# Half of the output columns moved beside the last delta rule heads, eight more merge columns in pairs, and early copies of transposed keys and values, in a one-core encoder layer

## The chip, the cores and the metric

The kernel runs on one NeuronCore of one Trainium2 chip, in one launch. The metric is the device time of one execution in microseconds. The kernel before takes 2275.59 us (median of three executions, 2275.45 to 2276.55).

## The reference, cut to what matters

One encoder layer is computed for 640 tokens (512 of a prompt, 128 of eight short requests), all in fp32, with 2048 channels:

```
z  = x @ w_in                      # q, k, v, gates, delta-rule q|k|v, two merge gates m_a, m_b (2048 columns each)
y_a = (fox_attention(...) * silu(gate_a)) @ w_out_fox      # 1024 -> 2048
y_b = (delta_rule(...)    * silu(gate_b)) @ w_out_gdn      # 1024 -> 2048
h  = (sigmoid(m_a) * y_a + sigmoid(m_b) * y_b) @ w_out
x1 = layer_norm(alpha * x + h)
out = x1 + sigmoid(x1 @ w_pl_gate) * rms_norm(p @ w_pl_proj)
```

The delta rule has 8 heads of width 128. Each head normalizes its queries and keys to unit length, scales keys and values by factors of its tokens, solves small triangular systems in blocks of 128 tokens, and carries a state from block to block.

## The kernel before, in words

**Columns.** Activations lie with channels on the 128 partitions and the 640 tokens along the free dimension, as 16 tiles (the list `self.op`). A "column" is 128 output channels: `column` runs 16 steps, one for each 128 input channels, and each step has 6 matmuls (`mm6`, L307 and L308). The 6 come from fp32 being split in two parts, high and low (weights `wh`, `wl`, activations `xh`, `xl`): high times high, high times low, low times high, each in two halves of 320 tokens. A column is 96 matmuls of 128x320 and needs 1 MB of weights. The two accumulators of a column lie in two of four PSUM banks `g`.

**Pairs.** Columns computed by `pair` (L381) are done two at a time by Strassen's scheme on 2x2 blocks, with 7 products in place of 8: 168 matmuls of 128x320 for two columns in place of 192. VectorE forms sums of weight halves (L243) and of results. In the kernel before 4 pairs are attention gate columns and 6 pairs are merge columns, that is 12 of the 32 merge columns (`FRONT`); they run in the first stage, while nothing else needs TensorE.

**Weights.** `w_ahead` runs before every step. It starts the DMA of the next half column (512 KB, L223, issued on SyncE) into one of three `wr` buffers, and splits pieces of it (four steps of a column) on ScalarE (`wh`, L253) and VectorE (`wl`, L254), at most five pieces ahead of TensorE.

**Lanes.** Work beside the columns is written as generators that a list of lanes steps once for every step of a column (`tick`). The engines execute in the order in which this planner writes instructions; it estimates the time of VectorE and ScalarE, but waits in the program are for the real results. In the delta rule stage (`phase_gdn`), each head has 4 columns (query, key, value, gate) and one merge column as filling (`FILL`); after head 7 there are 8 merge columns, beside which the chain of head 7 runs, and 2 more that load and split the 16 operand tiles of the output columns from DRAM (`ogd`).

**The delta rule of one head.** `gdn` transposes the keys (tile `pk`, L779, four 128x128 blocks of the prompt), then one block each of keys, values and queries (`pd`, L784 to L786), then four of queries (`pq`, L792), through four small PSUM banks `s`. The sums of squares (L781, L787, L788, L794) come straight from PSUM on ScalarE. VectorE then makes the inverse roots and the factors `cs` (L816 to L825). Only then ScalarE copies the keys out of `pk` and `pd`, scaled by `cs` (L829 to L831), and TensorE transposes the values (`pv`, L835), which ScalarE copies scaled (L837). The end of the previous head (`gdn_out`: L934, L938) takes two banks of the same four in between. `gdn_blocks` and `gdn_chunks` follow in other lanes.

**Output columns.** `tail` runs 16 columns with 16 steps each: steps 0 to 7 are the attention half, steps 8 to 15 the delta rule half, each in its own pair of banks. After each half VectorE multiplies the accumulator by its merge gate (L1511, two instructions of 128x320), and adds both (L1517). The gates come from DRAM (`md`, two tiles of 320 KB for each column, L1490). Then follow 16 columns with `w_out` and 16 with `w_pl_gate`.

Of the kernel before, what the change touches and what calls it, by code (L numbers as in the profile page):

```python
# [47 lines left out]
class Kernel:  # L48
# [8 lines left out]
    FRONT = 32 - 13 - 7  # L57
# [252 lines left out]
    def column(self, cols=1, each=None, groups=((0, 16),), after=None, modk=False, done=None):  # L310
# [6 lines left out]
        for n0, n1 in groups:  # L317
            ps = [tuple(self.gps(x.stop - x.start) for x in self.cut) for _ in range(cols)]
            for s in range(n0, n1):
                if each:  # L320
                    each(s)
                self.w_ahead()
                for x in range(cols):
                    self.mm6(ps[x], self.wk(c + x, s), self.op[(s - n0) % KT if modk else s], s == n0, s == n1 - 1)
# [445 lines left out]
    def gdn(self, h, kq, v):  # L770
# [5 lines left out]
        junk = self.zt([P, P], "junk")  # L776
        pk = self.sps()
# [15 lines left out]
        for t in range(4):  # L793
            nc.scalar.activation(junk, pq[:, t * P:(t + 1) * P], AF.Square, accum_out=ss[:, 5 + t:6 + t])  # L794

# [30 lines left out]
        kt = self.zt([P, 5, P], "kt", 2)  # L826
        vr = self.zt([P, 5, P], "vr", 2)
        for t in range(4):
            nc.scalar.mul(kt[:, t, :], pk[:, t * P:(t + 1) * P], cs[:, 3, t:t + 1])  # L829
        nc.scalar.mul(kt[:, 4, :], pd[:, 0:P], cs[:, 3, 4:5])  # L830
        nc.scalar.mul(vr[:, 4, :], pd[:, P:2 * P], cs[:, 0, 4:5])  # L831
        yield 2
        pv = self.sps()
        for t in range(4):
            nc.tensor.transpose(pv[:, t * P:(t + 1) * P], v[:, t * P:(t + 1) * P], self.ident)  # L835
# [75 lines left out]
    def gdn_out(self, h, ob, cs):  # L911
# [30 lines left out]
        nc.sync.dma_start(out=self.ogd[8 + h], in_=og)  # L942
# [405 lines left out]
    def phase_gdn(self, conv, work):  # L1348
# [13 lines left out]
        for h in range(H):  # L1362
# [16 lines left out]
            for _ in range(self.FILL if h < 7 else 8):  # L1379
                self.mcol("cth")  # L1380
        self.paced = False
        nc.sync.dma_start(out=self.o["conv"], in_=self.tails)

        raw, nop = {}, [None] * KT
        kq = self.kqs[0]
        tiles = [kq[:, 0, :], kq[:, 1, :]]
        tiles += [self.zt([P, T], t, n, "ogr") for t, n in (("strip", 1), ("cy", 1), ("sg", 1), ("v", 1), ("dt", 1))]

        def load(k):
            raw[k] = tiles[k % 7]  # L1390
            nc.sync.dma_start(out=raw[k], in_=self.ogd[k])

        def each1(s):
            if s >= 9:
                load(s - 9)

        def after(s):
            nop[s] = self.split(raw[s])
            if s + 7 == 15:
                self.until(lambda: self.gdone == 7)  # L1400
            if s + 7 < KT:
                load(s + 7)
        self.mcol("cth", each=each1)
        self.mcol("cth", after=after)
        self.op = nop

    def proj(self, m, op):
# [7 lines left out]
        self.column(groups=tuple((2 * g, 2 * g + 2) for g in range(8)), modk=True, done=fin)  # L1415
# [22 lines left out]
    def rstd(self, acc1, acc2, eps, out, mean=None):  # L1438
# [16 lines left out]
        if acc1 is not None:  # L1455
            m = self.zt([P, 160], "rm")
# [24 lines left out]
    def tail(self):  # L1481
# [5 lines left out]
        def load(n):  # L1487
            for x in range(2):
                ld[n, x] = self.zt([P, T], "ld", 4, "sab")
                nc.sync.dma_start(out=ld[n, x], in_=self.md[2 * n + x])  # L1490
# [3 lines left out]
        for n in range(16):  # L1494
            def each(s):
                if s == 1 and n < 15:
                    load(n + 1)
                if s == 1 and n == 1:
                    self.work["gens"].append(self.rstd(None, re, RMS_EPS, re))

            def after(s):
                if n == 15 and s % 3:
                    k = s - 1 - s // 3
                    nop[k] = self.split(mg[k])
            sab = [ld[n, 0], ld[n, 1]]

            def gated(ps):
                x = sab[len(gs)]
                gs.append(x)
                for hf, sl in enumerate((a, b)):  # L1510
                    nc.vector.scalar_tensor_tensor(out=x[:, sl], in0=x[:, sl], scalar=1.0, in1=ps[hf],  # L1511
                                                   op0=ALU.add, op1=ALU.mult)
            gs = []
            self.column(groups=((0, 8), (8, 16)), each=each, after=after, done=gated)
            sa, sb = gs
            m = self.zt([P, T], "m", 16, "mg")
            nc.vector.tensor_tensor(out=m, in0=sa, in1=sb, op=ALU.add)  # L1517
            mg.append(m)
# [7 lines left out]
        def xload(n):  # L1526
            xr[n] = self.zt([P, T], "ld", 4, "xr")
# [19 lines left out]
        for n in range(16):  # L1547
            def each(s):
                if n == 0 and s < 6:
                    nop[10 + s] = self.split(mg[10 + s])  # L1550
# [39 lines left out]
        def eload(n):  # L1590
            el[n] = self.zt([P, T], "ld", 4, "el")
# [108 lines left out]
def _layout(a):  # L1700
# [30 lines left out]
    bl += list(_wblock(np.concatenate([a["w_out_fox"][0], a["w_out_gdn"][0]], 0)))  # L1731
# [68 lines left out]
```

## Time and profile before

| | |
|---|---|
| median of 3 executions | 2275.59 us |
| the profiled execution's own time | 2279.4 us |
| its span, first to last instruction | 2277.6 us |
| mean granted TensorE clock | 0.998 |
| TensorE busy | 2257.4 us |
| VectorE busy | 1292.8 us |
| ScalarE busy | 802.7 us |
| mean DMA rate over the span | 129 GB/s |

In a profile PE is TensorE's matmuls, PEld its weight loads, DVE VectorE, ACT ScalarE, POOL GpSimd and SP SyncE, which issues all DMAs here. Times of rows are us from the start of the span, durations of one instruction ns. In a group `out<-in` names the tiles, `xN` counts instructions; "idle before" is the time in which the engine stood still ahead of them, followed by what ended it. A row of the waits names the waiting instruction, the one it waited for, the sum in us, how often, and the longest. Busy TensorE time is modelled, since matmuls overlap: a 128x320 matmul lasts 0.31 us and the next one starts about 0.15 us after it.

The stages by time: front columns to 99 us, pairs from 99 to 347 us, attention to about 740 us, then a projection, delta rule heads from 770 to about 1430 us, merge columns beside the end of head 7 to 1590 us, output columns from 1590 to 1815 us, then `w_out` and `w_pl_gate`.

### The profile page before, as it was taken

Reading aid. Unit: us, or ns where it says so; the run is one execution under the profiler, and the core shown is the slowest. Engines: PE = TensorE matmul, PEld = TensorE weight load, DVE = VectorE, ACT = ScalarE, POOL = GpSimd, SP = SyncE. Lnnn points to the kernel's source line nnn. Section 1 sums busy time; section 2 is a strip of 40 time slices with the busy share of each in tenths; the row PEclk is TensorE's granted clock in tenths of the full one; section 3 lists DMA queues with packets and bytes.
Section 4 is the critical chain, followed back from the end, with each engine's and each line's share of the span. In section 5 each row is a group of like instructions: output and inputs, shape, how many; then the busy total and the mean of one; then the engine's idle time right before and its main releaser. Section 6 shows DMA issues by size and latency. Waiting matters only on the chain. (4 is left out here: it accounts for less than half of the span.)

```text
span 2277.6 us, 39935 instructions
## 1 busy us (share of the span) xinstructions
PE 2257.4 (99%) x16034; PEld 2168.6 (95%) x16034; DVE 1292.8 (57%) x2787; ACT 802.7 (35%) x1782; POOL 63.6 (3%) x230
## 2 busy tenths in 40 slices
PE   9999999999999999999999999999999999999999
PEld 7899998978899999999999999999999999999999
DVE  5867664343444547667667667555433533657665
ACT  4444443333333543344344344324111311333222
POOL 0000000000000000000000000000000000020000
PEclk9999999999999999999999999999999999999999
DMA  6333336555654522232233332335433332323331
GB/s 224 125 114 103 123 126 219 201 198 196 198 184 163 182 87 95 91 114 95 95 108 101 97 99 92 115 108 208 150 124 123 104 106 96 100 88 115 121 121 69
DMA packets 114057, 294.72 MB, mean 129 GB/s; under 512 B 22201, under 2 KB 30473, under 8 KB 113873
## 3 DMA queue, kind: packets, MB, share of 16 engines
q1 hardware_dynamic: 113872, 292.18, 38.7%
q8 instruction: 126, 2.06, 0.4%
q14 instruction: 59, 0.48, 0.1%
HBM read 245.23 MB, written 46.90 MB: 128 GB/s over the span
## 5 line engine op out<-in xcount | busy, mean ns | idle before, releaser
L254 DVE TENSOR_TENSOR wl<-wr,wh 128x512 fp32r<-128x512 f32 x564 | 386.9, 691 | 556.1 <-ACT wh L253 542.1
L307 PE MATMUL g<-xh,wh 128*128 128x320 f32 (+1 forms) x1840 | 595.4, 324 | 0.2 <-ACT wh L253 0.2
L307 PE MATMUL g<-xl,wh 128*128 128x320 f32 (+1 forms) x1840 | 569.8, 310 | 0.6 <-DVE xl L282 0.6
L308 PE MATMUL g<-xh,wh 128*128 128x320 f32 x1840 | 569.3, 309 | 0.0
L308 PE MATMUL g<-xl,wh 128*128 128x320 f32 x1840 | 569.1, 309 | 0.0
L307 PE MATMUL g<-xh,wl 128*128 128x320 f32 (+1 forms) x1840 | 569.0, 309 | 0.0
L308 PE MATMUL g<-xh,wl 128*128 128x320 f32 x1840 | 568.5, 309 | 0.0
L253 ACT CAST wh<-wr 128x512 fp32r<-128x512 f32 x564 | 346.8, 620 | 619.8 <-PE g L308 545.9
L307 PEld LDWEIGHTS g<-xh,wh 128*128 128x128 f32 x1840 | 347.3, 189 | 17.6 <-issue 12.7
L307 PEld LDWEIGHTS g<-xl,wh 128*128 128x128 f32 x1840 | 347.0, 189 | 1.1 <-DVE xl L282 1.1
L308 PEld LDWEIGHTS g<-xh,wh 128*128 128x128 f32 x1840 | 347.0, 189 | 0.7
L308 PEld LDWEIGHTS g<-xl,wh 128*128 128x128 f32 x1840 | 346.9, 189 | 0.0
L307 PEld LDWEIGHTS g<-xh,wl 128*128 128x128 f32 x1840 | 346.4, 188 | 0.1
L308 PEld LDWEIGHTS g<-xh,wl 128*128 128x128 f32 x1840 | 346.0, 188 | 0.0
L381 PE MATMUL g<-xh,wh 128*128 128x320 f32 x320 | 99.0, 309 | 1.2 <-ACT u L391 1.2
L381 PE MATMUL g<-xh,wl 128*128 128x320 f32 x320 | 99.0, 309 | 0.0
L381 PE MATMUL g<-xl,wh 128*128 128x320 f32 x320 | 98.9, 309 | 0.0
L254 DVE TENSOR_TENSOR wl<-sr,wh 128x512 fp32r<-128x512 f32 x80 | 53.9, 690 | 41.1 <-ACT wh L253 40.9
L881 DVE TENSOR_TENSOR sx<-sx,sx 80x240 f32<-80x240 f32 (+14 forms) x240 | 68.3, 284 | 8.2
L879 DVE TENSOR_TENSOR sx<-sx,lanes 80x240 f32<-80x240 f32 (+14 forms) x240 | 67.8, 282 | 4.7
L1511 DVE SCALAR_TENSOR_TENSOR sab<-sab,g 128x320 f32<-128x320 f32 x64 | 28.3, 484 | 69.2 <-PE g L307 64.3
L751 DVE SCALAR_TENSOR_TENSOR cy<-strip,taps,cy 128x664 f32<-128x664 f32 x72 | 66.2, 920 | 1.3
(386 smaller groups left out, 2720.3 us busy)
## 6 DMA issues: line engine op xcount, KB each, us to landing
wr<-in_w SPq DMA_DIRECT2D x280, 512.0 KB
kc<-in_kc SPq DMA_DIRECT2D x32, 512.0 KB
vc<-in_vc SPq DMA_DIRECT2D x32, 512.0 KB
xr<-in_xT SPq DMA_DIRECT2D x32, 320.0 KB
md<-m SPq DMA_DIRECT2D x32, 320.0 KB
sab<-md SPq DMA_DIRECT2D x32, 320.0 KB
sr<-in_w SPq DMA_DIRECT2D x10, 512.0 KB
ogd<-og SPq DMA_DIRECT2D x16, 320.0 KB
```

The costliest lines, as they stand in the source:

```text
L253: nc.scalar.copy(out=hi, in_=src)
L254: nc.vector.tensor_tensor(out=lo, in0=src, in1=hi.bitcast(F32), op=ALU.subtract)
L307: nc.tensor.matmul(ps[0], whl[w], xhl[o][:, a], start=(first and x == 0), stop=(last and x == 2))
L308: nc.tensor.matmul(ps[1], whl[w], xhl[o][:, b], start=(first and x == 0), stop=(last and x == 2))
L381: nc.tensor.matmul(ps, a[:, w], b, start=(k == 0 and n == 0 and not more), stop=(k == 7 and n == 2), skip_group_check=True)
L751: nc.vector.scalar_tensor_tensor(out=y[:, 0:CV], in0=strip[:, i:i + CV], scalar=tp[:, 4 * ct + i:4 * ct + i + 1], in1=y[:, 0:CV], op0=ALU. ...
L879: nc.vector.tensor_tensor(out=tmp[:, :, 0:n], in0=xo[:, :, j:j + 1].to_broadcast([80, 8, n]), in1=lanes[:, j:j + 1, j + 1:32].to_broadcast ...
L881: nc.vector.tensor_tensor(out=x[:, :, j + 1:32], in0=xo[:, :, j + 1:32], in1=tmp[:, :, 0:n], op=ALU.subtract)
L1511: nc.vector.scalar_tensor_tensor(out=x[:, sl], in0=x[:, sl], scalar=1.0, in1=ps[hf], op0=ALU.add, op1=ALU.mult)
```

## The change

It has four parts.

1. `FRONT` goes from 12 to 20: 20 merge columns run as 10 pairs, so there are 14 pairs in place of 10.
2. The 8 merge columns after head 7 are gone. The two that load and split operands move to right behind head 7, and split the 8 attention tiles alone (`take`, three tiles of staging in turn). Then 8 weight columns follow, each of which holds the attention halves of two output columns (16 steps in two groups of 8, on operands 0 to 7). ScalarE copies each result out of PSUM (`kept`), and a DMA writes it to DRAM (`fd`). Meanwhile each delta rule tile is loaded and split when its head is done; head 7's goes from VectorE straight into the operand list.
3. `tail` has 8 weight columns in place of 16, with the delta rule halves of two output columns each (operands 8 to 15). For every group of 8 steps it loads three tiles (attention result and two gates) in place of two for 16 steps; VectorE gates the attention result ahead of the end of the group, then the other result, and adds. Eight of the 16 merged tiles are split along the way.
4. In `gdn` ScalarE copies transposed keys and values out of PSUM at once and unscaled (128x512 in one instruction), takes the keys' sums of squares from that copy, and scales keys and values in place in SBUF once `cs` is there. The transposes of the values stand ahead of the factors. There are more steps between these parts.

```diff
-    FRONT = 32 - 13 - 7
+    FRONT = 32 - 5 - 7
...
         pk = self.sps()
         for t in range(4):
             nc.tensor.transpose(pk[:, t * P:(t + 1) * P], kq[:, 0, t * P:(t + 1) * P], self.ident)
-        for t in range(4):
-            nc.scalar.activation(junk, pk[:, t * P:(t + 1) * P], AF.Square, accum_out=ss[:, t:t + 1])
+        nc.scalar.copy(out=kt[:, 0:4, :], in_=pk.rearrange("p (a b) -> p a b", b=P))
         yield
...
-        nc.scalar.activation(junk, pd[:, 0:P], AF.Square, accum_out=ss[:, 4:5])
+        nc.scalar.copy(out=kt[:, 4, :], in_=pd[:, 0:P])
+        nc.scalar.copy(out=vr[:, 4, :], in_=pd[:, P:2 * P])
         nc.scalar.activation(junk, pd[:, 2 * P:3 * P], AF.Square, accum_out=ss[:, 9:10])
+        yield
+        for t in range(5):
+            nc.scalar.activation(junk, kt[:, t, :], AF.Square, accum_out=ss[:, t:t + 1])
         yield
         pq = self.sps()
...
+        yield
+        pv = self.sps()
+        for t in range(4):
+            nc.tensor.transpose(pv[:, t * P:(t + 1) * P], v[:, t * P:(t + 1) * P], self.ident)
+        nc.scalar.copy(out=vr[:, 0:4, :], in_=pv.rearrange("p (a b) -> p a b", b=P))
...
-        for t in range(4):
-            nc.scalar.mul(kt[:, t, :], pk[:, t * P:(t + 1) * P], cs[:, 3, t:t + 1])
-        nc.scalar.mul(kt[:, 4, :], pd[:, 0:P], cs[:, 3, 4:5])
-        nc.scalar.mul(vr[:, 4, :], pd[:, P:2 * P], cs[:, 0, 4:5])
-        yield 2
-        pv = self.sps()
-        for t in range(4):
-            nc.tensor.transpose(pv[:, t * P:(t + 1) * P], v[:, t * P:(t + 1) * P], self.ident)
-        for t in range(4):
-            nc.scalar.mul(vr[:, t, :], pv[:, t * P:(t + 1) * P], cs[:, 0, t:t + 1])
-        yield 3
+        yield 2
+        for t in range(5):
+            nc.scalar.mul(kt[:, t, :], kt[:, t, :], cs[:, 3, t:t + 1])
+        for t in range(5):
+            nc.scalar.mul(vr[:, t, :], vr[:, t, :], cs[:, 0, t:t + 1])
+        yield 2
...
-            for _ in range(self.FILL if h < 7 else 8):
+            for _ in range(self.FILL if h < 7 else 0):
                 self.mcol("cth")
...
+        def kept(ps):
+            t = self.zt([P, T], ("strip", "cy")[self.nf % 2], 1, "fx")
+            for hf in range(2):
+                nc.scalar.copy(out=t[:, hf * HALF:(hf + 1) * HALF], in_=ps[hf])
+            nc.sync.dma_start(out=self.fd[self.nf], in_=t)
+            self.nf += 1
+        for n in range(8):
+            def each(s):
+                while n == 0 and due and (due[0][0] <= self.now or due[0][1] <= s):
+                    take()
+                k = 8 + n
+                if s == 1 and n < 7:
+                    self.until(lambda: self.gdone >= n)
+                    load(k, ("sg", "cth")[n % 2])
+                if s == 13 and n < 7:
+                    nop[k] = self.split(raw[k])
+            self.column(groups=((0, 8), (8, 16)), base=0, each=each, done=kept)
...
+            for x, d in enumerate((self.fd[n], self.md[2 * n], self.md[2 * n + 1])):
+                ld[n, x] = self.zt([P, T], "ld", 6, "sab")
+                nc.sync.dma_start(out=ld[n, x], in_=d)
...
+        def gated(ps):
+            n = len(mg)
+            x = ld[n, 2]
+            for hf, sl in enumerate((a, b)):
+                nc.vector.scalar_tensor_tensor(out=x[:, sl], in0=x[:, sl], scalar=1.0, in1=ps[hf],
+                                               op0=ALU.add, op1=ALU.mult)
+            m = self.zt([P, T], "m", 16, "mg")
+            nc.vector.tensor_tensor(out=m, in0=ld[n, 0], in1=x, op=ALU.add)
+            mg.append(m)
+        for u in range(8):
             def each(s):
-                if s == 1 and n < 15:
+                n = 2 * u + s // 8
+                if s % 8 == 0 and n < 15:
                     load(n + 1)
+                if s % 8 == 3:
+                    y, x = ld[n, 0], ld[n, 1]
+                    nc.vector.scalar_tensor_tensor(out=y, in0=x, scalar=1.0, in1=y, op0=ALU.add, op1=ALU.mult)
...
+            self.column(groups=((0, 8), (8, 16)), base=8, each=each, after=after, done=gated)
```

Two places show what this does to the order of the instructions. The first is TensorE in head 6, where the end of an earlier head (transposes of `ob`) meets the transposes of head 6; `s` are the four small banks, `kq` keys and queries, `v` values. Before:

```order
L934 MATMUL s<-cb,ob 128x128 x4
L938 MATMUL s<-cb,ob 128x128
L307 MATMUL g<-xh,wh 128x320
L308 MATMUL g<-xh,wh 128x320
L307 MATMUL g<-xl,wh 128x320
L308 MATMUL g<-xl,wh 128x320
L307 MATMUL g<-xh,wl 128x320
L308 MATMUL g<-xh,wl 128x320
L835 MATMUL s<-cb,v 128x128 x4
```

and now, at the same head:

```order
L938 MATMUL s<-cb,ob 128x128 x4
L942 MATMUL s<-cb,ob 128x128
L307 MATMUL g<-xh,wh 128x320
L308 MATMUL g<-xh,wh 128x320
L307 MATMUL g<-xl,wh 128x320
L308 MATMUL g<-xl,wh 128x320
L307 MATMUL g<-xh,wl 128x320
L308 MATMUL g<-xh,wl 128x320
L798 MATMUL s<-cb,kq_9131 128x128 x4
```

The values' transposes stood six matmuls behind the two transposes of `ob`; now the queries' transposes stand there, and the values' come 12 matmuls later. ScalarE in the same head, from the squares of the transposed queries on, before:

```order
L794 ACTIVATE junk,ss<-s 128x128 x4
L803 ACTIVATE dt<-dt 128x640
L804 ACTIVATE gr<-gr 128x640
L253 CAST wh<-wr 128x512
L812 CAST hl<-kq_8107 128x512
L829 ACTIVATE kt<-s,cs 128x128 x4
L830 ACTIVATE kt<-s,cs 128x128
L831 ACTIVATE vr<-s,cs 128x128
L253 CAST wh<-wr 128x512
L837 ACTIVATE vr<-s,cs 128x128 x4
```

and now, from the first copy out of the banks on:

```order
L783 COPY kt<-s 128x512
L789 COPY kt<-s 128x128
L790 COPY vr<-s 128x128
L791 ACTIVATE junk,ss<-s 128x128
L253 CAST wh<-wr 128x512
L794 ACTIVATE junk,ss<-kt 128x128 x5
L800 ACTIVATE junk,ss<-s 128x128 x4
L253 CAST wh<-wr 128x512
L805 COPY vr<-s 128x512
L253 CAST wh<-wr 128x512
L814 ACTIVATE dt<-dt 128x640
L815 ACTIVATE gr<-gr 128x640
```

Reads of `s` that waited for `cs` are gone from ScalarE; the scalings by `cs` (L839, L841, five of each) stand further on and read SBUF. The second place is SyncE at the start of the output columns; `fd` and `md` are attention results and gates in DRAM, `wr` weights. Before:

```order
L1490 DMA sab<-md_89 128x640
L1490 DMA sab<-md_90 128x640
L223 DMA wr<-in_w 128x1024 x2
L1490 DMA sab<-md_91 128x640
L1490 DMA sab<-md_92 128x640
L223 DMA wr<-in_w 128x1024 x2
```

and now:

```order
L1525 DMA sab<-fd_17208 128x640
L1525 DMA sab<-md_89 128x640
L1525 DMA sab<-md_90 128x640
L223 DMA wr<-in_w 128x1024
L1525 DMA sab<-fd_17209 128x640
L1525 DMA sab<-md_91 128x640
L1525 DMA sab<-md_92 128x640
L223 DMA wr<-in_w 128x1024
```

Between two half columns of weights there are now three loads in place of one on average.

More of the change, by code (lines that the diff above doesn't have):

```diff
@@ L308, in mm6, with column @@
             nc.tensor.matmul(ps[1], whl[w], xhl[o][:, b], start=(first and x == 0), stop=(last and x == 2))
-    def column(self, cols=1, each=None, groups=((0, 16),), after=None, modk=False, done=None):
+    def column(self, cols=1, each=None, groups=((0, 16),), after=None, base=None, done=None):
         c = self.col
@@ L776, in gdn @@
         junk = self.zt([P, P], "junk")
+        kt = self.zt([P, 5, P], "kt", 2)
+        vr = self.zt([P, 5, P], "vr", 2)
         pk = self.sps()
@@ L1414, in fin @@
             n[0] += 1
-        self.column(groups=tuple((2 * g, 2 * g + 2) for g in range(8)), modk=True, done=fin)
+        self.column(groups=tuple((2 * g, 2 * g + 2) for g in range(8)), base=0, done=fin)
         self.op = keep
```

84 lines of the change are left out of this document (40 added, 44 removed).

## The prediction

> **What bounds the kernel now.** I read the page first, then TensorE's waits, then the timeline around the longest of them, then the clock and the DMA rate by windows.
>
> ```profile
> span 2277.6 us, 39935 instructions
> PE 2257.4 (99%) x16034; PEld 2168.6 (95%) x16034; DVE 1292.8 (57%) x2787; ACT 802.7 (35%) x1782; POOL 63.6 (3%) x230
> PE   9999999999999999999999999999999999999999
> PEclk9999999999999999999999999999999999999999
> ```
>
> TensorE works in every fortieth of the span at nearly full clock; VectorE has 43% of its time free, ScalarE 65%. So time is matmuls, and what is to be gained is matmuls left out and TensorE's waits. These are its waits, all of them (us in total, times, longest):
>
> ```profile
> PE s L835 <- ACT kt L829: 5.4, 2, 3.2
> PE s L938 <- ACT junk L794: 3.4, 4, 1.3
> PE s L703 <- DVE xs L570: 2.3, 1, 2.3
> PE wu L1167 <- DVE z L1164: 1.2, 1, 1.2
> PE g L381 <- ACT u L391: 1.2, 1, 1.2
> PE s L1054 <- DVE rp L1050: 0.7, 2, 0.4
> PE g L307 <- DVE xl L282: 0.6, 2, 0.3
> PE g L307 <- ACT wh L253: 0.2, 1, 0.2
> ```
>
> They are 15 us in all. The two at the top, 8.8 us, are in the delta rule heads, where the change rewrites the order. L835 are the value transposes, which need a bank that the keys still occupy; L829 is the copy of the keys out of it, scaled by `cs`. The longer of the two, on TensorE's timeline:
>
> ```profile
> 1343.54 0.31 PE L308 MATMUL g<-xh,wl 128*128 128x320 f32 x1
> 1347.07 0.66 PE L835 MATMUL s<-cb,v 128*128 128x128 f32 x4 [3.21 <-ACT kt L829]
> ```
>
> and ScalarE's waits that belong to it:
>
> ```profile
> ACT kt L829 <- DVE cs L821: 28.4, 8, 3.8
> ```
>
> In all 8 heads ScalarE stands before L829 until VectorE has the factors, 3.6 us each on average. In two heads TensorE gets to L835 within that time. What follows the wait is in the next view: TensorE's granted clock in the first row after it, then in the same time at full clock (us, busy time and instructions of each engine, clock, DMA share, GB/s).
>
> ```profile
> 1348.03:1351.44 3.41, 3.41 (x15) 3.41 (x14) 1.61 (x3) 2.15 (x8) 0.00 (x0) 0.50 0.29 96
> 1351.44:1354.85 3.41, 3.41 (x26) 3.41 (x26) 0.69 (x1) 0.18 (x1) 0.00 (x0) 1.00 0.98 311
> ```
>
> For 3.41 us the clock is 0.50, and 15 matmuls run in place of 26. The wait of 3.2 us thus costs another 11 x 0.147 = 1.6 us.
>
> **The change part by part.** The sum is made against the profiled execution's own 2279.4 us, which is 3.8 us over the median 2275.59; I take the 3.8 off at the end.
>
> Eight merge columns go, four pairs come. The price of a column comes from the output columns, where nothing interrupts, and of a pair from the pairs themselves:
>
> ```profile
> L1511 DVE SCALAR_TENSOR_TENSOR sab<-sab,g x64: 478/482/489, 1597.9 to 1814.8; 128x320 f32<-128x320 f32 x64
> L381 PE MATMUL g<-xh,wl x320: 305/309/318, 99.6 to 347.3; 128*128 128x320 f32 x160
> ```
>
> L1511 has two instructions after each group of 48 matmuls: (1814.8 - 1597.9 - 0.5) / 31 = 6.98 us for a group, 0.1454 us for a matmul. L381's row runs from the third matmul of the first pair to the last of the tenth: 247.7 us less the wait of 1.2 us for 1677 matmuls, 0.1470 us each, so 24.7 us for a pair. Off: 8 x 96 = 768 matmuls at 0.1454 to 0.147 us, 111.7 to 112.9 us. On: 4 x 168 = 672 at 0.147, 98.8 us. Gain 12.9 to 14.1 us; I take 13.4. VectorE and ScalarE hide under the pairs as they do now: the page shows no wait in ten pairs but the one at the start, so six merge pairs of the same kind ran without one.
>
> The eight weight columns that take the place of merge columns beside head 7, and the eight left of sixteen output columns, have as many matmuls as the sixteen before: 0 us on TensorE. What they add lies beside: ScalarE copies 32 halves of 128x320, SyncE issues 16 stores and 16 loads of 320 KB. ScalarE is 65% free, and its weight casts run far ahead of need. What a late cast would mean is in the rivals.
>
> Early copies. A bank of keys is now free one copy after its transposes; in the new order at least 42 matmuls, 6 us, stand between the copies and the next user of their bank, where 5 stood between L829 and L835, and 1 or 2 between the squares and L938. The L835 waits go: 5.4 us. The half clock goes with the longer one: 1.6 us. The L938 waits have the same cause at one remove (with the keys' banks held, `ob` gets the bank of the queries, whose squares had only just been written), and go too: 3.4 us. What is late next: the steps of the state chain, whose two waits at L1054 are 0.7 us, 0.35 us each. In the new order more of them stand close behind what they read (six within ten matmuls, three before); I charge 3 more, 1.0 us, between 0 and 8 of them, 2.8 us.
>
> ScalarE's added work per head: two 512-wide and two 128-wide copies. Its squares of keys and its scalings now read SBUF in place of PSUM. The nearest rows, squares from PSUM and SBUF, scalings from PSUM and SBUF:
>
> ```profile
> L794 ACT ACTIVATE junk<-s x32: 277/278/279, 831.2 to 1426.6; 128x128 f32<-128x128 f32 x32
> L919 ACT ACTIVATE junk<-ob x40: 293/311/323, 971.5 to 1561.7; 128x128 f32<-128x128 f32 x40
> L829 ACT ACTIVATE kt<-s,cs x32: 359/368/378, 839.4 to 1434.8; 128x128 f32<-128x128 f32 x32
> L929 ACT ACTIVATE ob<-ob,rfy x40: 385/389/405, 978.9 to 1566.4; 128x128 f32<-128x128 f32 x40
> ```
>
> 33 and 21 ns more for each. Fifteen of them in a head come to 0.4 us, 3 us over 8 heads, in the place of the 28.4 us that ScalarE stood still: 0 us. The ten scalings in a row hold ScalarE for up to 10 x 0.389 = 3.9 us; no transposes or chain steps stand there in the order, and weight pieces are ahead.
>
> [...]
>
> Sum: 13.4 + 5.4 + 1.6 + 3.4 - 1.0 = 22.8 us off 2279.4 gives 2256.6 us, and less 3.8, **2252.8 us**. With the ends of the bounds 2250 to 2256 us.
>
> The start of the output columns. The store of the last result must land before the loads of the new stage are issued. The same happens now, with the last gate:
>
> ```profile
> 1591.33 0.32 SPq L1345 DMA_DIRECT2D md<-m  x1
> 1593.77 0.32 SPq L1492 DMA_DIRECT2D re<-sqd  x1
> 1594.14 1.85 SPq L1490 DMA_DIRECT2D sab<-md  x4
> 1597.86 0.89 DVE L1511 SCALAR_TENSOR_TENSOR sab<-sab,g 128x320 f32<-128x320 f32 x2 [4.72 <-PE g L308]
> ```
>
> 2.4 us from store to next load, and data 3.7 us later without a wait for it. Now VectorE asks for the first two tiles three steps (2.6 us) into the group, not at its end, so it may stand for some 5 us. Behind it are weight pieces that TensorE needs up to 14 us later (four pieces of 3.5 us) and the accumulators, needed 7 us after the group: no price.
>
> **The rivals.**
>
> *Waits come back in new places (0.15).* ScalarE takes instructions in order, and two or three steps of the chain get caught behind the ten scalings or behind the previous head's. For it: the same engine is the releaser of both waits that go. Against it: at the places named the order leaves 42 matmuls. Price by the rows L703 and L835, 2.3 to 3.2 us, with the half clock 1.6 us more: one or two, 4 to 8 us, 2257 to 2261 us. [...] The trace goes further: after L703's 2.3 us, too, the clock was 0.5, as part of this window shows.
>
> ```profile
> 345.00:370.00 25.00, 25.00 (x173) 23.97 (x172) 9.85 (x19) 9.50 (x22) 2.25 (x5) 1.00 0.75 253
> 370.00:385.00 15.00, 12.71 (x78) 10.45 (x78) 5.33 (x15) 2.86 (x9) 0.24 (x1) 0.89 0.63 226
> ```
>
> *The wait at L703 goes as well (0.07).* It stands at the start of the attention, where weights, keys and values load at once. The order from the last pair on is unchanged, so the load meets the same queue; if it does come out otherwise, 2.3 + 1.6 us more are gained: 2249 us.
>
> *Head 7 ends late, or the pairs pay less (0.05).* Head 7 must be done before the eighth operand of the first output group. In the order its last transposes stand 97 matmuls, 14 us, ahead of that use. If VectorE fell behind by more, splits and chain competing, TensorE would wait for the rest, some 6 us: 2259 us.
>
> *The output columns become bound by DMA, and the kernel slower (0.03).* A group of 6.98 us now needs three tiles of 320 KB and 512 KB of weights, 1.47 MB, 211 GB/s, where that stage now moves
>
> ```profile
> 1600.00:1815.00 215.00, 215.00 (x1469) 214.24 (x1468) 90.15 (x160) 45.78 (x75) 0.00 (x0) 1.00 0.38 122
> 1537.00:1594.00 57.00, 57.00 (x397) 56.54 (x397) 28.93 (x59) 27.60 (x61) 0.00 (x0) 1.00 0.60 208
> ```
>
> 122 GB/s. To eat the 22.8 us, each of 16 groups must take 1.43 us longer, that is the rate must be below 1.47 MB / 8.41 us = 175 GB/s; at 165 GB/s it would be 8.9 us a group, 31 us in all, and the end 2284 us. Against it: the second row (208 GB/s, TensorE never idle), and the 253 GB/s above, also without idle time in that window. For it: right behind those 253 GB/s weights did come late, as ScalarE's waits from 340 to 380 us have it:
>
> ```profile
> ACT wh L253 <- DMA wr<-in_w: 11.4, 2, 6.0
> ```
>
> So the stage would have to get less than was moved there, at a rate that was held for 25 us.
>
> **How the numbers follow.** My forecast has 0.70. The range from 2247 to 2261 us holds the forecast's own bounds, the L703 case, the late head and nearly all of the first rival. A measurement of this kernel can tell 0.2%, 4.6 us, from no change. All cases but the DMA one lie 14 us or more below 2275.59: faster 0.95; slower 0.03; same 0.02 for a mishap that sums up several of these.
>
> **What would show it.** Right: ten pairs become fourteen at 24.7 us each (the row of L381 ends near 446 us); TensorE's waits for small banks in the heads are gone from its list, and so is the half clock there; output groups stay at 6.98 us. Wrong: a wait over 1 us anywhere in the heads; SyncE or VectorE's loads of `sab` ahead of TensorE's waits in the output columns; a merge pair over 25 us.

## The result, and the profile after

The changed kernel takes 2252.45 us (median of four executions, 2250.86 to 2256.83), the kernel before beside it 2276.07 us (2275.45 to 2278.19): ratio 0.9898, 95% interval 0.9881 to 0.9915. The forecast was 2252.8 us. The profiled execution is the longest of the four, 2256.83 us against 2279.4 before: 22.6 us less, where the sum had 22.8. That is closer than the sum deserves: two of its zeros and one of its terms were off, and that their errors cancelled is luck.

The page of the kernel after, its span and busy times:

```profile
span 2255.0 us, 39956 instructions
PE 2240.8 (99%) x15938; PEld 2154.1 (96%) x15938; DVE 1328.8 (59%) x2831; ACT 842.7 (37%) x1874; POOL 68.3 (3%) x230
```

TensorE has 96 matmuls less, as 768 off and 672 on make it, VectorE and ScalarE some 40 us more work. The whole list of TensorE's waits after:

```profile
PE s L704 <- DVE xs L571: 3.8, 1, 3.8
PE s L1512 <- DVE rym L1506: 1.6, 1, 1.6
PE wu L1174 <- DVE z L1171: 1.2, 1, 1.2
PE g L382 <- ACT u L392: 1.1, 1, 1.1
PE s L1020 <- ACT xx L1016: 0.5, 1, 0.5
PE g L307 <- ACT wh L253: 0.4, 1, 0.4
PE g L307 <- DVE xl L282: 0.3, 1, 0.3
```

The waits for value transposes and for the end of the previous head are gone (8.8 us), and those at the state chain's L1054; in the heads only 0.5 us at L1020 is new. The wait at the start of the attention (L703, now L704) is 3.8 us in place of 2.3. And there is one at a place where the forecast had none: L1512, the inverse roots of the embedding, in the first output columns.

The pairs end where they should. One group of their matmuls, duration and first and last start:

```profile
L382 PE MATMUL g<-xh,wl x448: 305/309/318, 99.1 to 445.5; 128*128 128x320 f32 x150
```

346.4 us for fourteen pairs, 24.7 us each, as before. The windows around the wait at L704 (TensorE's clock is the third figure from the right):

```profile
473.53:476.94 3.41, 0.46 (x4) 0.20 (x2) 0.89 (x2) 0.87 (x2) 0.00 (x0) 1.00 0.55 220
476.94:480.36 3.42, 2.60 (x11) 1.88 (x15) 1.73 (x5) 1.01 (x4) 0.00 (x0) 0.50 0.15 30
480.36:483.77 3.41, 3.41 (x16) 2.15 (x9) 1.31 (x3) 0.00 (x0) 0.24 (x1) 0.50 0.37 133
```

Two periods of half clock follow, 6.8 us, where before one of 3.4 us did. From the last pair to the first key transposes it is 478.8 us before and 481.4 after: 2.7 us that the sum did not have. The other new wait, on the way from SyncE to TensorE:

```profile
1676.58 0.32 SPq L1426 DMA_DIRECT2D fd<-fx  x1
1678.83 0.32 SPq L1527 DMA_DIRECT2D re<-sqd  x1
1679.18 0.43 SPq L1525 DMA_DIRECT2D sab<-fd  x1
1679.98 0.79 SPq L1525 DMA_DIRECT2D sab<-md  x2
...
1687.04 0.83 DVE L1546 SCALAR_TENSOR_TENSOR sab<-sab 128x640 f32<-128x640 f32 x1 [9.25 <-DMA sab<-fd]
...
1690.64 0.32 DVE L1502 TENSOR_SCALAR rv<-s 128x160 f32<-128x160 f32 x1
1694.79 0.82 DVE L1506 TENSOR_TENSOR rym<-rqy,cb 128x640 f32<-128x640 f32 x1
...
1695.67 1.35 PE L1512 MATMUL s<-rym,cb 128*128 128x320 f32 x4 [1.61 <-DVE rym L1506]
```

VectorE stands 9.3 us for the first tiles of the new stage, not some 5. The forecast went by the 3.7 us from issue to data that the stage took before, with four tiles issued in a row; with six it was 7.9 us (1679.18 to 1687.04). Behind that wait VectorE has weight pieces, the gating and then the chain of the inverse roots, 4.97 us from L1502 to the end of L1506, and TensorE comes to L1512 1.6 us too early. The weight pieces and accumulators, which the forecast named as cover, were in time; it did not name the chain of the roots, which the change starts 8 steps sooner than before.

### The profile page after: what moved, and what is told of

It reads as the page before. It is cut to its first block, busy times and chain, and to the rows that moved or that the text cites. A ratio compares the mean times of both kernels' runs of the same rounds, so it can differ in the third digit from the quotient of the medians.

```text
span 2255.0 us, 39956 instructions
## 1 busy us (share of the span) xinstructions
PE 2240.8 (99%) x15938; PEld 2154.1 (96%) x15938; DVE 1328.8 (59%) x2831; ACT 842.7 (37%) x1874; POOL 68.3 (3%) x230
## 4 chain that ended last, share of the span: by engine, by line
PE 95%; DVE 2%; DMA 2%; ACT 1%; issue 0%; SPq 0%; ACTq 0%; DVEq 0%
PE g L307 34%; PE g L308 33%; PE g L382 15%; PE g L351 3%; PE s L659 1%; PE s L713 1%; PE s L616 1%; PE o L351 1%; PE s L852 1%; DMA wr<-in_w 0%; PE s L989 0%; PE s L704 0%; DMA kc<-in_kc 0%; DVE wl L254 0%; DVE xr L1231 0%
## 5 line engine op out<-in xcount | busy, mean ns | idle before, releaser
L254 DVE TENSOR_TENSOR wl<-wr,wh 128x512 fp32r<-128x512 f32 x556 | 380.8, 690 | 523.5 <-ACT wh L253 496.9
L307 PE MATMUL g<-xh,wh 128*128 128x320 f32 (+1 forms) x1712 | 555.7, 325 | 0.6 <-ACT wh L253 0.4
L253 ACT CAST wh<-wr 128x512 fp32r<-128x512 f32 x556 | 341.1, 619 | 511.4 <-PE g L308 427.9
L307 PE MATMUL g<-xl,wh 128*128 128x320 f32 (+1 forms) x1712 | 530.0, 310 | 0.3 <-DVE xl L282 0.3
L307 PE MATMUL g<-xh,wl 128*128 128x320 f32 (+1 forms) x1712 | 529.2, 309 | 0.0
L307 PEld LDWEIGHTS g<-xh,wh 128*128 128x128 f32 x1712 | 323.0, 189 | 17.6 <-issue 12.7
L308 PEld LDWEIGHTS g<-xh,wh 128*128 128x128 f32 x1712 | 323.0, 189 | 0.7
L307 PEld LDWEIGHTS g<-xl,wh 128*128 128x128 f32 x1712 | 322.8, 189 | 0.7 <-DVE xl L282 0.7
L308 PEld LDWEIGHTS g<-xl,wh 128*128 128x128 f32 x1712 | 322.6, 188 | 0.0
L307 PEld LDWEIGHTS g<-xh,wl 128*128 128x128 f32 x1712 | 322.0, 188 | 0.1
L308 PEld LDWEIGHTS g<-xh,wl 128*128 128x128 f32 x1712 | 321.8, 188 | 0.0
L254 DVE TENSOR_TENSOR wl<-sr,wh 128x512 fp32r<-128x512 f32 x112 | 75.7, 690 | 62.3 <-ACT wh L253 62.0
L253 ACT CAST wh<-sr 128x512 fp32r<-128x512 f32 x112 | 67.8, 617 | 68.2 <-PE g L382 68.2
L382 PEld LDWEIGHTS g<-xh,wh 128*128 128x128 f32 x448 | 84.2, 188 | 1.4 <-ACT u L392 1.4
L382 PEld LDWEIGHTS g<-xh,wl 128*128 128x128 f32 x448 | 84.3, 188 | 0.0
L382 PEld LDWEIGHTS g<-xl,wh 128*128 128x128 f32 x448 | 84.1, 188 | 0.0
```

What stands on the lines that cost most here:

```text
L253: nc.scalar.copy(out=hi, in_=src)
L254: nc.vector.tensor_tensor(out=lo, in0=src, in1=hi.bitcast(F32), op=ALU.subtract)
L307: nc.tensor.matmul(ps[0], whl[w], xhl[o][:, a], start=(first and x == 0), stop=(last and x == 2))
L308: nc.tensor.matmul(ps[1], whl[w], xhl[o][:, b], start=(first and x == 0), stop=(last and x == 2))
L382: nc.tensor.matmul(ps, a[:, w], b, start=(k == 0 and n == 0 and not more), stop=(k == 7 and n == 2), skip_group_check=True)
```

## The experiments

Theory: the gain has two independent parts, fewer matmuls (columns) and banks that come free earlier (early copies), and the waits at L704 and L1512 have causes of their own. The rivals were that the waits of the heads only move, and that the moved halves gain or lose something by themselves. Each kernel was timed beside the kernel before on the same chip; ratios are to that.

**The early copies alone.** The kernel before with the new `gdn`, and nothing else (the diff of `gdn` above).

> The kernel before with the new order inside the delta rule heads alone (early unscaled copies, values transposed ahead of the factors, scaling in place in SBUF); columns, pairs and output columns as before. Theory (the keys' banks were held until the factors were there): TensorE's waits for the value transposes (5.4 us in two heads) and for the end of the previous head (3.4 us in four) both go, and with the longer of them 3.4 us of half clock (1.6 us); at most 1 us of new waits. Own time 9.4 to 10.4 us under the kernel before, some 2266 us, and the wait at the start of the attention stays at 2.3 us. Rival (ScalarE takes instructions in order, so waits move to other places behind its ten scalings): TensorE's list has new rows of 1 us and more in the heads, and the gain is 5 us or less, 2271 us or more.

2265.59 us, before 2277.4, ratio 0.9953 (0.9939 to 0.9966). TensorE's whole list:

```profile
PE s L703 <- DVE xs L570: 3.2, 1, 3.2
PE wu L1170 <- DVE z L1167: 1.2, 1, 1.2
PE g L381 <- ACT u L391: 1.1, 1, 1.1
PE g L307 <- ACT xh L281: 1.1, 1, 1.1
PE g L307 <- DVE xl L282: 0.5, 2, 0.3
PE s L1016 <- ACT xx L1012: 0.5, 1, 0.5
```

The theory holds: nothing of 1 us is left or new in the heads (the 1.1 us at L307 is ahead of them). The gain is 10.7 us by the ratio. By the trace, from the first key transposes to a matmul in the middle of `w_out`, it is 1104.4 us before and 1091.9 here, 12.5 us: 9.0 of listed waits (8.8 gone and 0.7 at L1054, 0.5 new), 1.6 of half clock, and 1.9 that no wait explains: TensorE's idle time in that stretch is 9.5 us before and 0.5 here, as listed, so these 1.9 us lie in the spacing of the matmuls themselves, and their cause is not shown. The wait at L703 is 3.2 us with the order ahead of it unchanged: its length is a matter of the execution, not of the change.

**The columns alone.** The changed kernel with `gdn` as it was.

> The changed kernel with the old order inside the heads: only the columns move (four more pairs, attention half of the output columns beside the last heads). Theory: the gain of the columns is 13.4 us (768 matmuls off, 672 on), less the 1.6 us that TensorE waits for the inverse roots in the output columns and some 3 us of longer wait and half clock at the start of the attention: 8 to 12 us under the kernel before, 2264 to 2268 us. The waits for the value transposes and the end of the previous head are back in TensorE's list, 5 to 10 us in all, since heads 0 to 6 are written as before. Rival (the waits in the heads depend on what stands beside them, and the new neighbours of head 7 give it time): fewer than half of those waits come back, and the time is 2260 us or less.

2264.88 us, ratio 0.9944 (0.9932 to 0.9957), 12.8 us by the ratio. The head of TensorE's list:

```profile
PE s L836 <- ACT kt L830: 4.4, 2, 2.3
PE s L704 <- DVE xs L571: 3.4, 2, 3.2
PE s L939 <- ACT junk L795: 3.3, 4, 1.3
```

7.7 of the 8.8 us are back, with the same counts: the rival falls. 10.7 and 12.8 make 23.5 us, the whole change 23.2 by its ratio: the parts add up. There is no wait at L1512 here, with the same order of that stage: VectorE stood 7.4 us for the first tiles, not 9.3.

**One instruction of the early copies.** The kernel before, in which the four prompt blocks of the keys are copied out at once:

```diff
+        nc.scalar.copy(out=kt[:, 0:4, :], in_=pk.rearrange("p (a b) -> p a b", b=P))
...
-            nc.scalar.activation(junk, pk[:, t * P:(t + 1) * P], AF.Square, accum_out=ss[:, t:t + 1])
+            nc.scalar.activation(junk, kt[:, t, :], AF.Square, accum_out=ss[:, t:t + 1])
...
-            nc.scalar.mul(kt[:, t, :], pk[:, t * P:(t + 1) * P], cs[:, 3, t:t + 1])
+            nc.scalar.mul(kt[:, t, :], kt[:, t, :], cs[:, 3, t:t + 1])
```

> The kernel before with one small part of the early copies: the four prompt blocks of the keys are copied unscaled by one 128x512 copy right behind their transposes, squared from that copy and scaled in place; the fifth block, the values and all the order of the yields stay as before. Theory that one bank is enough for the wait at the end of the previous head: those 3.4 us go, and the wait ahead of the value transposes goes or shrinks, since they get the bank of the keys: 4 to 10 us under the kernel before. Rival (the fifth blocks' bank, held until the factors are there, now stands in the way instead, or the value transposes still come too early): the wait of 5.4 us stays within 2 us of what it was, and the gain is 4 us or less.

2269.88 us, ratio 0.9967 (0.9955 to 0.9978). The head of its list:

```profile
PE s L703 <- DVE xs L570: 3.3, 1, 3.3
PE s L1055 <- DVE rp L1051: 1.2, 2, 0.9
PE wu L1168 <- DVE z L1165: 1.2, 1, 1.2
```

Both waits of the heads are gone. One bank in time is enough: it was the keys' bank that was short, for the value transposes and, at one remove, for the end of the previous head. The state chain now waits 1.2 us, 0.5 more. By the ratios 7.5 of the 10.7 us come from this. By the traces, over the stretch from the first key transposes to the middle of `w_out`, it is 10.2 of 12.5 us; from the last pair to that stretch, where the order is the same, this profile is 2.8 us longer than the one of all early copies, with 6.8 us of half clock against none.

**The inverse roots later.**

```diff
-                if s == 9 and u == 0:
+                if s == 1 and u == 1:
                     self.work["gens"].append(self.rstd(None, re, RMS_EPS, re))
```

> The changed kernel with the inverse roots of the embedding started eight steps later, in the second half of the first output column instead of nine steps into it. Theory (VectorE stands 9.3 us for the first tiles of the new stage, and the chain of the inverse roots behind it reaches TensorE 1.6 us late): the wait of 1.6 us for the roots goes, nothing else changes, and the time falls by 1.6 us. Rival (the backlog of VectorE is passed on to whatever TensorE needs next): a wait of the same size stands at a weight piece or an accumulator of the second output column, and the time is the same.

(Eight steps later is one step into the second weight column, not in the first.) L1512 does not wait, and nothing takes its place. The end of VectorE's chain, and the matmuls that read it:

```profile
1696.86 0.82 DVE L1506 TENSOR_TENSOR rym<-rqy,cb 128x640 f32<-128x640 f32 x1
...
1700.17 1.24 PE L1512 MATMUL s<-rym,cb 128*128 128x320 f32 x4
```

2253.12 us, ratio 0.9894 (0.9881 to 0.9908). That L1512 doesn't wait would show little by itself, since it doesn't in most runs without the delay either; the margin shows the mechanism. Here the roots are ready 2.5 us ahead of TensorE. Undelayed they were 0.06 to 0.8 us ahead in the five profiles in which VectorE stood 6.7 to 7.5 us for the first tiles, and TensorE waited 1.6 and 2.1 us in the two in which it stood 9.3 and 9.6. The worth is not shown: the change ran at 0.9898 and, in a later run, 0.9886.

**The values of the first attention head later.** At the start of the attention SyncE has keys, values and weights to fetch; in the changed kernel (SyncE, then ScalarE):

```profile
463.92 4.85 SPq L223 DMA_DIRECT2D wr<-in_w  x3
...
475.12 0.62 ACT L253 CAST wh<-wr 128x512 fp32r<-128x512 f32 x1 [7.54 <-DMA wr<-in_w]
```

ScalarE stands 7.5 us for a weight piece, VectorE behind it (L254), and behind that the normalization for L704. The experiment moves the three loads of the values from 3 steps behind the keys to 16, and so behind two more loads of weights in SyncE's order.

```diff
-            yield 3
-            for j in range(3):
-                self.load_kv(0, "v", j)
-            yield 3
+            yield 6
...
-        yield (16 if h == 0 else 1)
+        if h == 0:
+            yield 10
+            for j in range(3):
+                self.load_kv(0, "v", j)
+            yield 6
+        else:
+            yield 1
```

> The changed kernel with the loads of the values for the first attention head (three of 512 KB) issued ten steps later, so that they no longer stand in SyncE's and the DMA engines' way when the first weights of the attention are fetched. In five profiled runs TensorE waited 2.3 to 3.8 us there (the normalization behind a weight piece behind a late weight load), and 0, 3.4 or 6.8 us of half clock followed. Theory (bytes queued ahead of those weights make them late): the wait falls below 2 us, no half clock follows, and the time is 2 to 6 us under the changed kernel, 2247 to 2251 us. Rival (the keys and the planned order of the weights alone make them late, or the values are now late for their own use): the wait stays at 2.3 to 3.8 us or stands in a new place, and the time is the same within 1 us or longer.

2250.91 us (2250.26 to 2251.27), ratio 0.9879 (0.9865 to 0.9892).

TensorE's longest wait, and ScalarE's weight piece ahead of the normalization:

```profile
PE s L619 <- DMA kc<-in_kc: 1.5, 1, 1.5
```

```profile
469.20 0.62 ACT L253 CAST wh<-wr 128x512 fp32r<-128x512 f32 x1 [2.20 <-DMA wr<-in_w]
```

ScalarE now waits 2.2 us for that piece in place of 7.5 (6.0 in the later run of the changed kernel), the wait at L704 is gone, and no half clock follows; in its place TensorE waits 1.5 us for keys. So the mechanism is as the theory had it. Its worth is not shown: the gain over the change, 1.5 us between medians, is below what the expectation had, and inside the intervals. What did shrink is the scatter: 1.0 us between executions, where the change had 6.0 and 2.2.

**One pair more.** The two merge columns behind the attention go into a fifteenth pair.

```diff
-    FRONT = 32 - 5 - 7
+    FRONT = 32 - 3 - 7
...
-        for _ in range(2):
-            self.mcol("sc")
```

> The changed kernel with one more pair: the two merge columns behind the attention go into the pairs (15 in place of 14). Theory (a pair is 24 matmuls less than two columns, at 0.146 us each): 3.5 us less, 2249 us. Rival (the two columns are the cover of the attention's last steps, and without them TensorE waits for the last head's result): a new wait of 3 us or more in TensorE's list ahead of the projection, and the time is the same or longer.

2276.92 us, ratio 0.9994 (0.9985 to 1.0003): all of the change's gain is gone. Its waits of over 1.5 us, and the window at the end of the attention:

```profile
PE s L704 <- DVE xs L571: 9.8, 3, 7.3
PE s L616 <- DMA kc<-in_kc: 3.0, 1, 3.0
PE g L307 <- ACT ph L1334: 2.8, 1, 2.8
PE s L638 <- DVE xd L571: 2.3, 1, 2.3
PE s L713 <- ACT pT L706: 1.7, 3, 0.7
```

```profile
825.00:865.00 40.00, 21.34 (x138) 13.96 (x137) 12.93 (x33) 9.06 (x24) 0.00 (x0) 0.65 0.47 156
```

A pair saves some 3.4 us, but the columns that it replaces covered the last steps of the attention: 18.7 us of idle time stand between 825 and 865 us, and the clock is 0.51 from 830 to 858 us and 0.96 from there to 900, in all some nine periods of 3.41 us at half clock. The rival was right, by far more than it had asked.

**The end of head 7 without cover.** The kernel before with twenty merge columns in pairs, and nothing beside the rest of head 7.

```diff
-    FRONT = 32 - 13 - 7
+    FRONT = 32 - 5 - 7
...
-            for _ in range(self.FILL if h < 7 else 8):
+            for _ in range(self.FILL if h < 7 else 0):
                 self.mcol("cth")
+        self.until(lambda: not conv["gens"] and self.gdone == 7)
```

> The kernel before with twenty merge columns in pairs, as in the change, but without the moved attention halves: nothing stands beside the rest of head 7, which runs as fast as its own waits allow, and the output columns stay as they were. It asks what the move of the halves is worth. Theory (the halves gain nothing by themselves, they are the cover that lets the merge columns leave): the pairs' 13.4 us are lost again, since TensorE waits in head 7's chain for 30 to 80 us, partly at half clock, and the time is 2290 to 2345 us. Rival (head 7's chain is short when nothing else is in its way): TensorE waits less than 13 us in it, and the time is 2276 us or less.

2329.86 us, ratio 1.0228 (1.0213 to 1.0243). TensorE in the stretch of head 7's chain, and around it:

```profile
1470.00:1520.00 50.00, 47.49 (x344) 45.87 (x343) 40.37 (x112) 21.46 (x66) 2.42 (x12) 1.00 0.30 97
1520.00:1610.00 90.00, 51.73 (x310) 37.77 (x311) 48.57 (x189) 22.62 (x79) 4.41 (x14) 0.51 0.17 52
1610.00:1640.00 30.00, 30.00 (x206) 30.00 (x205) 15.25 (x22) 15.19 (x25) 0.00 (x0) 1.00 0.78 275
```

38 us without a matmul, and a mean clock of 0.51 over these 90 us. Against the columns alone, where the halves stand there, it is 51.9 + 12.8, some 65 us by the ratios. That is what the moved halves are worth as cover; as work they are worth nothing: the merge columns can only leave because these take their place.

**Every load of the output columns twice.**

```diff
                 nc.sync.dma_start(out=ld[n, x], in_=d)
+                nc.sync.dma_start(out=self.zt([P, T], ("acc2", "cm", "rs")[x], 1, "dd"), in_=d)
```

> The changed kernel with every load of the output columns' three tiles issued a second time, into tiles that nothing reads: six tiles of 328 KB and 524 KB of weights in a group of 6.98 us, 357 GB/s in place of 216. It tells how far the changed kernel is from the rate that decides. Theory (the rate ends somewhere above 253 GB/s, the highest that was held for 25 us before): at 253 GB/s a group takes 9.8 us, 43 us more over 15 groups, at 311 GB/s (the highest of a window of 3.4 us) 8.0 us, 15 us more. So 15 to 43 us over the changed kernel, 2267 to 2296 us. Rival (transfers are far from their limit here): groups stay at 6.98 us and the time within 3 us.

2253.56 us, ratio 0.989 (0.9874 to 0.9905). The same 90 us after the change, and with all loads twice:

```profile
1700.00:1790.00 90.00, 90.00 (x616) 90.00 (x615) 56.34 (x90) 22.59 (x37) 0.00 (x0) 1.00 0.65 218
```

```profile
1700.00:1790.00 90.00, 90.00 (x616) 90.00 (x615) 56.50 (x90) 22.58 (x37) 0.00 (x0) 1.00 0.97 365
```

365 GB/s in place of 218, the same 616 matmuls, 7.0 us for a group of 48 in both. Only the wait at L1512 is longer, 2.1 us. The rival was right: the change leaves at least 40% of the rate unused.

**Twenty waits put in.** In ten `w_out` columns, twice each:

```diff
+        def stall(k):
+            p0, p1 = self.sps(), self.sps()
+            nc.tensor.transpose(p0[:, 0:P], mg[0][:, 0:P], self.ident)
+            nc.vector.tensor_copy(out=st[:, 0:P], in_=p0[:, 0:P])
+            for _ in range(k):
+                nc.vector.tensor_tensor(out=st, in0=st, in1=st, op=ALU.max)
+            nc.tensor.transpose(p1[:, 0:P], st[:, 0:P], self.ident)
+            nc.scalar.copy(out=st[:, 0:P], in_=p1[:, 0:P])
```

> The changed kernel with twenty waits put in: in ten of the w_out columns TensorE transposes a block, VectorE copies it and does one, two or three operations of 0.82 us on it, and TensorE transposes the result, so it stands for some 1.5 to 3.5 us at different moments. It asks when a wait is followed by half clock. In the runs so far a wait of 3.2 us was followed by none, one of 2.3 us by 3.4 us of it and one of 3.2 us by 6.8 us. Theory (the clock is set for periods of one grid of 3.41 us, by how long TensorE stood still inside the period before): half clock follows where 2.0 us or more of one period are idle and not where 1.87 us or less are, whatever the wait's whole length. Rival (the length of the wait decides): half clock follows all waits over some length and none below it, wherever they lie on the grid. The time is 40 to 80 us longer.

2324.54 us in its one execution, 20 waits of 46.5 us in all. Two of the same length, each with the periods of the grid in which it lies and the one after:

```profile
1832.32 0.30 PE L1590 MATMUL s<-cb,st 128*128 128x128 f32 x1 [2.22 <-DVE st L1589]
...
1861.34 0.39 PE L1590 MATMUL s<-cb,st 128*128 128x128 f32 x1 [2.21 <-DVE st L1589]
```

```profile
1827.29:1830.71 3.42, 2.81 (x20) 2.54 (x18) 1.65 (x4) 0.62 (x1) 0.00 (x0) 1.00 0.00 0
1830.71:1834.12 3.41, 1.80 (x13) 1.83 (x14) 1.43 (x2) 0.27 (x1) 0.00 (x0) 1.00 0.52 159
1834.12:1837.53 3.41, 3.41 (x25) 3.41 (x24) 0.69 (x1) 0.62 (x1) 0.00 (x0) 1.00 0.00 0
1858.01:1861.43 3.42, 1.21 (x10) 0.96 (x9) 2.54 (x4) 0.54 (x1) 0.00 (x0) 1.00 0.32 91
1861.43:1864.84 3.41, 3.41 (x14) 3.41 (x15) 0.00 (x0) 0.27 (x1) 0.00 (x0) 0.50 0.43 159
```

The first is cut by a period's end into 0.6 and 1.6 us and costs nothing more; the second lies inside one period, and 14 matmuls run in the next one in place of 25. Of the twenty, eight had 1.98 to 2.66 us inside one period, and half clock followed all eight; twelve had 1.90 or less, and it followed none. Three waits of 3.1 us, cut in two near their middle, had none; three others of 3.1 us, cut less evenly, had it, and so had four of 2.2 us. Length alone does not decide.

**Both delays, and the change again.** The two diffs above together, beside the changed kernel on the same chip.

> The changed kernel with both delays: the first attention head's values loaded ten steps later, and the inverse roots of the embedding started eight steps later. Theory (the two waits have nothing to do with each other): TensorE waits less than 2 us at the start of the attention, without half clock, and not at all for the inverse roots; 4 to 6 us under the changed kernel run beside it, 2247 to 2249 us. Rival (the wait for the roots is only passed on, and the first one is worth 2 us at most): within 2 us of the changed kernel.

> The changed kernel as it is, beside the one with both delays, for a comparison on the same chip: 2251 to 2254 us. Where its waits at the start of the attention (2.3 to 3.8 us so far) and for the inverse roots fall on the grid of 3.41 us is different in every execution, so each execution may lose 0, 1.7 or 3.3 us to half clock. Rival (half clock belongs to the place and not to the moment): 6.8 us of half clock at the start of the attention in this profile as in the first.

Both delays: 2250.91 us (2250.37 to 2251.26), ratio 0.988 (0.9864 to 0.9897); full clock throughout, no wait for the roots, 2.0 us for keys. The change again: 2252.11 us (2251.13 to 2253.31), ratio 0.9886 (0.9871 to 0.99). 1.2 us between medians is less than this measurement tells apart, and less than the theory's 4 to 6. The change's wait at L704 was 3.0 us this time, with one period of half clock, not two: the moment decides, not the place.

## Why the prediction was right, point by point

- *Columns, 13.4 us.* Right. Four pairs came at 98.7 us (forecast 98.8). In the columns alone the stage from the first key transposes fell from 1104.4 to 989.2 us; less 1.0 us of shorter waits and 1.6 of half clock that this execution lacks, 112.6 us for 768 matmuls, forecast 111.7 to 112.9. The halves on TensorE cost 0, as said.
- *Waits at L835 and L938, 8.8 us.* Right, with the bank as the cause, which the kernel with one early copy shows.
- *Half clock, 1.6 us.* Right for the execution that was profiled, but as a price of a wait it is a chance: 2.3 us came without it (the columns alone) and 3.2 us as well (the early copies alone).
- *New waits in the heads, 1.0 us.* Too high: 0.5 us came, and the 0.7 us at L1054 went. With the 1.9 us that no wait explains the early copies gave 12.5 us by the trace where the sum had 9.4, 3.1 us more.
- *Start of the output columns, "no price".* Wrong in the profiled execution, by 1.6 us. The step that failed is the list of what is queued behind VectorE's wait: it had weight pieces and accumulators, and not the inverse roots. The term "some 5 us" for that wait was too small as well: it took 6.7 to 9.6 us in the nine profiles with this stage. So VectorE's wait for `sab` did stand ahead of one of TensorE's, which the forecast had named as a sign of being wrong.
- *The wait at L703 stays as it is.* The order is unchanged, but the wait is not one number: 1.8 to 3.8 us in ten profiles where the loads ahead of it are the same, with 0 to 6.8 us of half clock; with ten pairs ahead 2.3 to 3.3 us, with fourteen 1.8 to 3.8, so the change is not seen in it. What makes it differ between executions stays open. From 2.3 and 3.4 it went to 3.8 and 6.8: 2.7 us against the sum.
- The three errors, 3.1 us for it and 4.3 against it, and 0.5 us each from the columns and from an earlier start, leave 22.6 against 22.8. Nothing tied them together.
- *Rivals.* Waits that move in the heads: none. L703 gone: only when the values load later. Head 7 late: no such wait. DMA: the point from which it decides, 175 GB/s, was sought far too near; 365 GB/s were moved for 90 us of the output columns, and TensorE did not wait in them. (The group's 1.47 MB counts a KB as 1024 bytes and a MB as 1000 KB; in the unit of the rates it is 1.51 MB, so 216 and 179 GB/s stand for the 211 and 175.)
- *ScalarE's added reads of SBUF, 0 us.* Right: in the changed kernel squares take 311 ns from SBUF and 277 from PSUM, scalings from SBUF 388 where they took 368 from PSUM, and no wait of 1 us came of it.

## What to carry to other kernels

Where a transposed tile waits in PSUM for factors that are not there yet, copy it out unscaled at once and scale it in SBUF: one 128x512 copy a head took away 8.8 us of waits in all, whose victims were other tiles' transposes. Work that fills another chain's gaps is priced by what happens without it: a pair that saves 3.4 us made the kernel 22 to 25 us longer, by the ratios, where it took the cover of the attention's end, and the moved halves, worth nothing as work, stand for 65 us. When a stage begins with loads, go through everything that is queued behind the engine that waits for them, the short chains too, before writing "no price".

## What the runs showed of the hardware

- In the traces of the kernels before and after, TensorE's clock changed only at whole multiples of 3.413 us from each other: the stretches of one clock last 372.05, 3.41, 965.97, 3.41 and 925.01 us before, which are 109, 1, 283, 1 and 271 times 3.413, and 471.04, 6.83 and 1768.10 us after, 138, 2 and 518 times. This grid lay otherwise in the two: counted from the first instruction its points stand 3.2 us past the multiples of 3.413 before, 2.5 us after. Half clock followed the periods with 2.30 and 2.45 us of idle time before (from 375.23 and 1344.62 us), with 2.95 us after (from 473.53 us), and with 2.20 and 2.66 us in the kernel with twenty waits (from 1858.01 and 1974.07 us). It followed none of those with 0.77 us before (from 1341.20 us), with 1.61 us after (the wait at L1512) and with 1.90 us in the kernel with twenty waits (the larger part of a wait of 3.1 us that ends at 1842.85 us). Idle time is not the whole rule: in the kernel with one more pair 1.6 us had it (the second part of a wait of 2.8 us that a period's end cuts, and one of 0.3 behind it, in the period that ends at 830.4 us). The wait of 3.2 us in the early copies alone, which a period's end cuts into 1.81 and 1.44 us (an expectation above has 1.87 for the first), came without half clock:

```profile
374.11:377.53 3.42, 1.61 (x11) 1.34 (x10) 0.55 (x1) 0.62 (x1) 0.00 (x0) 1.00 0.95 376
377.53:380.94 3.41, 1.97 (x15) 1.10 (x15) 2.07 (x7) 1.27 (x4) 0.00 (x0) 1.00 0.10 42
```

- A second half period followed where the first still held 0.8 us (after, from 476.94 us) and 2.45 us (twenty waits, from 1977.48 us) of idle time. None followed where it held nothing: twice before (from 378.64 and 1348.03 us) and once with twenty waits (from 1861.43 us). So a wait of 2 to 3.8 us costs itself and, by where it falls on the grid, 0, 1.7 or some 3 us more: an estimate, half of one period or of two, less half of what the wait itself takes of the second. That fits the scatter of some us between executions, and that it shrank to 1.0 us when the wait went; it was not tested further.
- The DMA engines moved 365 GB/s for 90 us, in the kernel with all loads twice (1700 to 1790 us), beside a TensorE that was busy for all 90 of them.
